# Seven-product weight groups in seven of eight places, and a down block's low part made by an accumulating GpSimd transfer

## The chip, the cores and the metric

The kernel runs on one core of one Trainium2 chip. The metric is the device time of one execution in microseconds (us). The engines are named as in the profile: PE is TensorE (PEld its weight loads), DVE is VectorE, ACT is ScalarE, POOL is GpSimd, SP is SyncE, which here only issues DMAs.

## What is computed

One decoder layer on 256 tokens of 2048 features, in float32: a SwiGLU with 5632 hidden features, a mixer of attention heads, and a second SwiGLU. The change touches the two SwiGLUs.

```python
def swiglu(x, w_gate, w_up, w_down):
    return (jax.nn.silu(x @ w_gate) * (x @ w_up)) @ w_down
...
h = h + 0.5 * swiglu(rms_norm(h, norm_ffn1_g[l]), ffn1_w_gate[l], ffn1_w_up[l], ffn1_w_down[l])
...
h = h + o @ w_out[l]
h = h + 0.5 * swiglu(rms_norm(h, norm_ffn2_g[l]), ffn2_w_gate[l], ffn2_w_up[l], ffn2_w_down[l])
```

## The kernel before

**A product.** A float32 value is kept as the sum of a rounded part ("hi", type fp32r) and what the rounding lost ("lo"). One product of a 128x128 block of activations with a 128x512 block of weights is three matmuls (`mm3`, lines 326 to 328): hi by hi, hi by lo, lo by hi. Weights arrive as float32, so each block of them has to be split: ACT casts it to hi, and DVE subtracts hi from the raw block to get lo.

**Units and down blocks.** A SwiGLU goes through 11 blocks of 512 hidden features. A *unit* (`unit`, line 589) computes gate and up of one block: it takes 8 weight groups of 128x2048, each 1 MB. A *down block* (`down`, line 679) takes 4 groups of 1 MB from `w_down` for one block and adds the result to h: ACT scales the sums into `st` (line 710), and GpSimd adds `st` to h in SBUF by an accumulating DMA of 512 KB (line 718). The order is unit 0, unit 1, down 0, unit 2, down 1, and so on; the last two down blocks are done together behind unit 10. A unit and the down block behind it are called a *round* here.

**Two kinds of groups.** A group of kind D (`whole`, line 391) is one load, one ACT cast and one DVE subtract of 128x2048, and 8 products. A group of kind S (`seven`, line 418) uses Winograd's form of a 2x2 block product: 7 products, for which DVE first forms sums of weight blocks (lines 437, 444, 445), ACT casts 1536 raw and 2048 summed columns in three pieces, and DVE subtracts twice (line 389, 1536 and 2048 columns). On the side of the activations the combinations are formed once for each pair of blocks (`form_of`, line 551) and kept in tiles `fu`. Behind a unit with S groups, DVE combines the sums in PSUM by eight operations of 128x512 (line 626), then comes the activation function (ACT, line 641, and DVE, line 649), the transposes (PE, line 507), and the split of the result into `hT` (ACT line 665, DVE line 389).

The table `UNITS` gives the kind of each group of each unit: 8 D in unit 0, then 3, 5, and from unit 3 on 6 S of 8.

**Buffers and order.** Three raw buffers of 1 MB (`raw` twice, and `rawx` in the first SwiGLU or `rawy` in the second), two for sums, five for hi and five for lo. An S group takes two of hi and two of lo, a D group one of each; a pair comes free when PE has used it. SP issues the loads in the order of the groups; a load waits until its raw buffer has been read for the last time.

The order of the instructions on every engine inside a SwiGLU is fixed by a planner (`arrange`, line 97): it goes through the tasks with a cost for each (`cast`, `sub`, numbers such as 0.69), a lag until the result can be used, and a due place counted in products, and writes down the order that comes out. The chip then waits on semaphores in that order; the costs themselves do nothing there.

Of the kernel before, what the change touches and what calls it, by code (L numbers as in the profile page):

```python
# [9 lines left out]
F32 = mybir.dt.float32  # L10
# [7 lines left out]
P = 128  # L18
# [25 lines left out]
F2_ORDER += [(2, "whiy", F32R)] * (NHI - 2 - FREE2) + [(3, "wloy", F32R)] * (NLO - 2 - FREE2) + [(0, "rawy", F32)] * (NRAW - 3)  # L44


# [30 lines left out]

LAG = 0.06
AHEAD = 60


def cast(n):
    return 0.2 + 0.00084 * n


def sub(n):
    return 0.16 + 0.00104 * n

# [8 lines left out]
def arrange(tasks, pools):  # L97
# [102 lines left out]
def hybrid_layer(ctx: ExitStack, tc: tile.TileContext, a: dict, out: bass.AP):  # L200
# [47 lines left out]
    cst = keep.tile([P, C_ONE], F32, name="cst")  # L248
    vec = keep.tile([P, V_END], F32, name="vec")
    pos = keep.tile([P, NT], I32, name="pos")  # L250

    hold.tile([P, 16], F32, name="pad")
    h = hold.tile([P, NT, D], F32, name="h")
    ident = cst[:, C_ID : C_ID + P]
    later = {}
    nc.scalar.dma_start(vec, a["vec"])

# [100 lines left out]
    def ffn(pool, u, wgu, wd, slots, banks, rstd, held=None, first=None, lead=None, done=None, out=None):  # L358
# [32 lines left out]
        def whole(src, pieces):  # L391
# [24 lines left out]
            return new, [(by[i * 512 // n], lambda i=i: cols(i)) for i in range(4)], {3: [("hi", c0), ("lo", l0)]}  # L416

        def seven(src):

# [48 lines left out]
        def group(kind, src, held, stat, need, form=None, pieces=1, last=False):  # L468

            new, w, free = seven(src) if kind == "S" else whole(src, pieces)  # L470
            n0 = len(main)
# [45 lines left out]
        def into_u(un, gcol, due):  # L517

            def finish(k, v, x):
                ends = []  # L520
                for j in range(2):
                    dst, gain = un(k + j), vec[:, gcol + k + j : gcol + k + j + 1]
                    c = task("act", 0.46, lambda j=j, dst=dst, gain=gain: nc.scalar.mul(dst[:, 0, :], v()[:, j], gain), [x], due)
                    l = task("dve", 0.48, lambda j=j, dst=dst, gain=gain: stt(
                        out=dst[:, 1, :], in0=v()[:, j], scalar=gain, in1=f32(dst[:, 0, :]), op0=ALU.mult, op1=ALU.subtract,
                    ), [c] + ends[-1:], due)
                    ends.append(l)
                    ready[k + j] = [c, l]
# [4 lines left out]
        def squares_of(ssq, c, need, due):  # L533

            ends = []
            for t in range(NT):
                q = task("act", 0.84, None, need[t], due, take={"sq": 1})
                q.give.append(("sq", q))
# [9 lines left out]
        forms = {}  # L548
        count = [k.count("S") for k in UNITS]

        def form_of(p, need, due):

            tile_, over = fu[p], u(2 * p)[:, :, P:SEQ]

# [34 lines left out]
        def unit(b):  # L589

            kinds, ns = UNITS[b], count[b]
            pair = {"S": iter(range(ns)), "D": iter(range(ns, 8))}
            held, hs, sq3 = {}, [], []
            for n, kind in enumerate(kinds):
                p = next(pair[kind])
                if b == 0 and first is not None:
                    first[0](p, task, ready)
                if kind == "S" and p not in forms:
                    fresh[p] = len(main)
                    form_of(p, used[p] + [x for k in (2 * p, 2 * p + 1) for x in ready.get(k, ())], len(main) - 4)  # L600
                n0 = group(
# [17 lines left out]
            if ns:  # L619
# [4 lines left out]
                def step(o_, key, in1, op, need, due, free=True):  # L624
                    return task(
                        "dve", 0.69, lambda: tt(out=o_(), in0=bank_of(held[key]), in1=in1(), op=op), need + [held[key]["last"]], due,
                        give=[("bank", held[key]["first"])] if free else (),
# [11 lines left out]
            for t in range(NT):  # L639
                src = (lambda t=t: s_tile()[:, t, :]) if ns else (lambda t=t: bank_of(R(t, 0)))  # L640
                a = task("act", 0.73, lambda t=t, src=src: nc.scalar.activation(
                    s_tile()[:, t, :], src(), AF.Silu, scale=rms[-1][:, t : t + 1]
# [6 lines left out]
                f = task("dve", 0.7, lambda t=t, src=src: stt(  # L649
                    out=s_tile()[:, t, :], in0=src(), scalar=rms[-1][:, t : t + 1], in1=s_tile()[:, t, :], op0=ALU.mult, op1=ALU.mult,  # L650
# [8 lines left out]
            def finish(k, v, x):  # L659
# [5 lines left out]
                c = task("act", cast(512), lambda: nc.scalar.copy(rows_tile()[:, :, 0, :], v()), [x], due + 4)  # L665
                l = task("dve", 0.69, lambda: low(rows_tile()[:, :, 1, :], v(), rows_tile()[:, :, 0, :]), [c], due + 4)
                row_ready[b, k // 2] = [c, l]
# [11 lines left out]
        def down(blocks, final):  # L679
# [21 lines left out]
        def settle(cp, held, final, later):  # L701

            due, c0, ends = len(main), 2 * cp * 512, []
            for t in range(NT):
                if not final:
                    pair = []
                    for j in range(2):
                        def run(t=t, j=j, pair=pair, held=held):
                            st = own("st", pair[0].got["st"][0], [P, 1024], F32)
                            nc.scalar.mul(st[:, j * 512 : j * 512 + 512], bank_of(held[t, j]), 0.5)  # L710
                        pair.append(task(
                            "act", 0.63, run, [held[t, j]["last"]] + pair, due + t + 4 * j, take={"st": 1} if j == 0 else (),
                            give=[("bank", held[t, j]["first"])],
# [100 lines left out]
    with tc.tile_pool(name="f1", bufs=1) as fp:  # L814
# [10 lines left out]
        def before(p, task, ready):  # L825
# [12 lines left out]
            for j in range(2):  # L838
                k = 2 * p + j
                gain = vec[:, V_G1 + k : V_G1 + k + 1]  # L840
                c = task("act", 0.46, lambda j=j, k=k, gain=gain: nc.scalar.mul(
                    u1(k)[:, 0, :], xs[i][:, p % 4, j], gain
                ), [ld], 8 * p - 4)
                l = task("dve", 0.48, lambda j=j, k=k, gain=gain: nc.vector.scalar_tensor_tensor(
                    out=u1(k)[:, 1, :], in0=xs[i][:, p % 4, j], scalar=gain, in1=f32(u1(k)[:, 0, :]),
# [32 lines left out]
    with tc.tile_pool(name="mix", bufs=1) as mp:  # L878
        ap_ = mp
        mst = mp.tile([P, C_END - C_ONE], F32, name="mst")  # L880
        nc.sync.dma_start(mst, a["cst"][:, C_ONE:])
        ones, tri = mst[:, :P], mst[:, C_TRI - C_ONE : C_TRI - C_ONE + P]
        m_swa, m_fox = (mst[:, C_MSK - C_ONE + i * SEQ :][:, :SEQ] for i in range(2))
# [54 lines left out]
        def rope_tables(name, gcol):  # L938
            g = vec[:, gcol : gcol + HD]
            ga = g[:, 0:32].unsqueeze(1).broadcast_to([P, NT, 32])  # L940
# [8 lines left out]
        nsink = ap_.tile([P, 32], F32, name="nsink")[:, :NH]  # L949
        nc.vector.tensor_scalar_mul(nsink, vec[:, V_SINK : V_SINK + NH], -1.0)  # L950

# [92 lines left out]
        def fox_mm(hf, i):  # L1044
# [10 lines left out]
        nc.vector.tensor_tensor(  # L1055
            out=z, in0=prs[:, :, 0:NH], in1=vec[:, V_BF : V_BF + NH].unsqueeze(1).broadcast_to([P, NT, NH]), op=ALU.add
        )
# [116 lines left out]
        def fox_rows(hf, i, pr, rf):  # L1174
# [3 lines left out]
            for t in range(NT):  # L1178
# [11 lines left out]
                for jj in range(2):  # L1190
                    bt = small_ps()
                    for j in range(4):
# [7 lines left out]
                        bt[0 : HD + 2, :].rearrange("p (j k) -> p j k", j=4),  # L1200
                        vec[0 : HD + 2, gcol : gcol + 1],
                    )
# [84 lines left out]
    with tc.tile_pool(name="f2", bufs=1, reuse_waits=REUSE) as fp:  # L1287
        slots, fu = [[], [], [], []], []
        for i, nm, dt in F2_ORDER:
            if i == 4:  # L1290
                fu += [fp.tile([P, 3, 2, P], F32R, name="fu%d" % p) for p in range(max(k.count("S") for k in UNITS))]
            else:
# [89 lines left out]
```

## Time and profile before

| what | us |
|---|---|
| median of 3 runs (lowest, highest) | 1747.77 (1747.45, 1747.9) |
| the profiled execution's own time | 1747.29 |
| its span, first to last instruction | 1745.0 |
| first SwiGLU, to its last transposes | about 0 to 684 |
| mixer | about 684 to 1054 |
| second SwiGLU | about 1054 to 1745 |

The span is what the profile covers; the 2.29 us around it are in the time alone. The page gives busy time by engine, a picture in 40 slices, the DMA queues, the chain of work that ended last, and the costliest groups of instructions. A busy PE is not a PE at its peak, since matmuls overlap: the distance from one start to the next is what counts. The same holds for DVE and ACT here, as the rows in the prediction show.

### The profile page before, as it was taken

Reading aid. Unit: us, or ns where it says so; the run is one execution under the profiler, and the core shown is the slowest. Engines: PE = TensorE matmul, PEld = TensorE weight load, DVE = VectorE, ACT = ScalarE, POOL = GpSimd, SP = SyncE. Lnnn points to the kernel's source line nnn. Section 1 sums busy time; section 2 is a strip of 40 time slices with the busy share of each in tenths; the row PEclk is TensorE's granted clock in tenths of the full one; section 3 lists DMA queues with packets and bytes.
Section 4 is the critical chain, followed back from the end, with each engine's and each line's share of the span. In section 5 each row is a group of like instructions: output and inputs, shape, how many; then the busy total and the mean of one; then the engine's idle time right before and its main releaser. Section 6 shows DMA issues by size and latency. Waiting matters only on the chain.

```text
span 1745.0 us, 21056 instructions
## 1 busy us (share of the span) xinstructions
PE 1734.7 (99%) x8052; PEld 1444.1 (83%) x8052; DVE 1510.2 (87%) x1640; ACT 1058.4 (61%) x1217; POOL 73.8 (4%) x94
## 2 busy tenths in 40 slices
PE   9999999999999999999999999999999999999999
PEld 6888888888888888998788888888888888888887
DVE  7899999998999996668777769799999999999994
ACT  7566566666666654655766656556666566656661
POOL 0000000000000000000000000000000000000000
PEclk9999999999999999999999999999999999999999
DMA  9676677678678664564444456577678578667763
GB/s 345 221 234 237 215 247 246 212 241 250 229 220 266 227 237 154 166 210 153 139 146 138 135 191 241 201 209 241 217 227 259 220 233 265 215 226 246 256 214 121
DMA packets 73141, 377.49 MB, mean 216 GB/s; under 512 B 7760, under 2 KB 16464, under 8 KB 39504
## 3 DMA queue, kind: packets, MB, share of 16 engines
q1 hardware_dynamic: 62064, 337.09, 53.8%
q0 software_dynamic: 10688, 38.80, 11.5%
q8 instruction: 63, 1.03, 0.2%
q14 instruction: 38, 0.31, 0.1%
q10 hardware_dynamic: 288, 0.25, 0.0%
HBM read 336.27 MB, written 2.10 MB: 194 GB/s over the span
## 4 chain that ended last, share of the span: by engine, by line
PE 98%; DMA 1%; DVE 0%; ACT 0%; issue 0%; SPq 0%; DVEq 0%
PE acc L327 25%; PE acc L326 25%; PE acc L328 25%; PE sm L328 6%; PE sm L326 6%; PE sm L327 6%; PE acc L507 1%; PE sm L1025 1%; PE sc L1214 1%; DMA rawx<-in_wgu 1%; PE sm L1031 1%; PE sm L1193 0%; PE sm L507 0%; DMA raw<-in_wgu 0%; PE sc L1139 0%; PE sm L1032 0%
## 5 line engine op out<-in xcount | busy, mean ns | idle before, releaser
L326 PE MATMUL acc<-whi,u 128*128 128x512 f32 (+1 forms) x690 | 263.4, 383 | 0.9 <-DVE s L989 0.9
L327 PE MATMUL acc<-wlo,u 128*128 128x512 f32 (+1 forms) x690 | 263.4, 382 | 0.6 <-DVE wlo L389 0.5
L328 PE MATMUL acc<-whi,u 128*128 128x512 f32 (+1 forms) x690 | 262.0, 381 | 0.0
L243 DVE TENSOR_TENSOR wlo<-raw,whi 128x1024 fp32r<-128x1024 f32 (+1 forms) x112 | 128.9, 1154 | 75.1 <-ACT whi L242 74.5
L242 ACT CAST whi<-raw 128x1024 fp32r<-128x1024 f32 (+1 forms) x112 | 111.0, 991 | 96.8 <-PE acc L328 88.1
L389 DVE TENSOR_TENSOR wlo<-raw,whi 128x1536 fp32r<-128x1536 f32 (+3 forms) x73 | 142.1, 1949 | 8.8 <-ACT whi L407 8.7
L326 PEld LDWEIGHTS acc<-whi,u 128*128 128x128 f32 x690 | 129.4, 188 | 24.0 <-DVE s L989 1.3
L327 PEld LDWEIGHTS acc<-wlo,u 128*128 128x128 f32 x690 | 129.5, 188 | 23.4 <-DVE wlo L389 1.4
L328 PEld LDWEIGHTS acc<-whi,u 128*128 128x128 f32 x690 | 129.4, 188 | 22.1 <-issue 0.8
L710 ACT ACTIVATE st<-acc 128x512 f32<-128x512 f32 x109 | 65.5, 601 | 82.3 <-PE acc L328 81.2
L389 DVE TENSOR_TENSOR wloy<-raw,whiy 128x1536 fp32r<-128x1536 f32 (+1 forms) x55 | 110.2, 2004 | 5.5 <-ACT whiy L407 5.5
L718 POOL DMA_DIRECT2D h<-st x72 | 62.4, 867 | 1212.8 <-ACT st L710 1110.0
L389 DVE TENSOR_TENSOR wlox<-raw,whix 128x2048 fp32r<-128x2048 f32 (+1 forms) x52 | 109.5, 2111 | 1.0 <-ACT whix L407 1.0
L389 DVE TENSOR_TENSOR wlo<-sums,whi 128x2048 fp32r<-128x2048 f32 x45 | 102.9, 2286 | 8.3 <-ACT whi L425 8.3
L437 DVE TENSOR_TENSOR sums<-raw 128x1024 f32<-128x1024 f32 x76 | 92.6, 1219 | 14.9 <-DMA raw<-in_wgu 14.9
L407 ACT CAST whi<-raw 128x2048 fp32r<-128x2048 f32 (+2 forms) x43 | 75.3, 1752 | 36.1 <-DMA raw<-in_wd 15.7
L407 ACT CAST whix<-raw 128x2048 fp32r<-128x2048 f32 x35 | 66.9, 1911 | 39.4 <-DMA raw<-in_wd 11.8
L327 PE MATMUL acc<-wlox,u 128*128 128x512 f32 x223 | 86.9, 390 | 0.5 <-DVE wlox L389 0.5
L328 PE MATMUL acc<-whix,u 128*128 128x512 f32 x223 | 86.8, 389 | 0.0
L326 PE MATMUL acc<-whix,u 128*128 128x512 f32 x223 | 86.8, 389 | 0.0
L389 DVE TENSOR_TENSOR wloy<-sums,whiy 128x2048 fp32r<-128x2048 f32 x34 | 77.7, 2286 | 4.4 <-ACT whiy L425 4.4
L327 PE MATMUL acc<-wloy,u 128*128 128x512 f32 x209 | 81.4, 390 | 0.1
(340 smaller groups left out, 4526.5 us busy)
## 6 DMA issues: line engine op xcount, KB each, us to landing
raw<-in_wgu SPq DMA_DIRECT2D x109, 1024.0 KB, 5.1
raw<-in_wd SPq DMA_DIRECT2D x65, 1024.0 KB, 4.8
h<-st POOLq DMA_DIRECT2D x72, 512.0 KB, 6.0
rawy<-in_wgu SPq DMA_DIRECT2D x33, 1024.0 KB, 4.8
rawx<-in_wgu SPq DMA_DIRECT2D x32, 1024.0 KB, 5.8
raw<-in_wf SPq DMA_DIRECT2D x48, 512.0 KB, 3.8
raw<-in_wo SPq DMA_DIRECT2D x32, 512.0 KB, 3.4
raw<-in_ws SPq DMA_DIRECT2D x32, 388.0 KB, 3.5
```

The source lines that it names most:

```text
L242: nc.scalar.copy(hi, src)
L243: nc.vector.tensor_tensor(out=lo, in0=src, in1=hi.bitcast(F32), op=ALU.subtract)
L326: nc.tensor.matmul(o, lhsT=shi, rhs=mhi, start=start, stop=False)
L327: nc.tensor.matmul(o, lhsT=shi, rhs=mlo, start=False, stop=False)
L328: nc.tensor.matmul(o, lhsT=slo, rhs=mhi, start=False, stop=stop)
L389: tt(out=o_, in0=a, in1=f32(b), op=ALU.subtract)
L407: c.run = lambda raw=raw, hi=hi: nc.scalar.copy(hi(), raw())
L437: tt(out=sm()[:, :1024].rearrange("p (j n) -> p j n", j=2), in0=v[:, 0:3:2, :], in1=v[:, 3:4, :].broadcast_to([P, 2, 512]), op=ALU.add,)
L507: nc.tensor.transpose(bt[:, j * SEQ + t * P : j * SEQ + (t + 1) * P], src()[:, t, m], ident)
L710: nc.scalar.mul(st[:, j * 512 : j * 512 + 512], bank_of(held[t, j]), 0.5)
L718: nc.gpsimd.dma_start(h[:, t, c0 : c0 + 1024], st, accum_op=ALU.add)
L1025: nc.tensor.transpose(bt[:, j * P : (j + 1) * P], src[:, j, :], ident)
```

## The change

Seven edits go together.

1. `UNITS` now has a table for each SwiGLU: 4, 6 and then 7 S groups in the first, 5, 6 and then 7 in the second. The number of `fu` tiles goes from 6 to 7.
2. The third group of each down block but the last two gets a new kind, L (`added_low`): ACT casts the raw block to hi and so frees the raw buffer; ACT writes minus hi into lo; a DMA from GpSimd then reads the same weight block from HBM a second time and adds it to lo in SBUF. DVE does nothing for this group.
3. The planner's costs for ACT and DVE are set lower, its general lag from 0.06 to 0.13.
4. The planner may take POOL's tasks out of order.
5. Room for the larger tiles: the scratch of GpSimd's DMAs goes from 2048 to 512 bytes of each partition, `vec` keeps only its first 64 columns, and the others (attention gains, sinks, forget bias) are loaded into a tile `own` of the mixer by one more DMA.
6. A padding tile goes from 16 to 56 columns.
7. Pairs of blocks are dealt to S and D groups through a table `PAIRS`, which leaves them as they were.

```diff
-UNITS = ["D" * 8, "DDSSDSDD", "DSSSSSDD"] + ["SDSSSSSD"] * (NB - 3)
+UNITS = [["D" * 8, x, "DSSSSSSD"] + ["SSSDSSSS"] * (NB - 3) for x in ("DDSSDSSD", "DSSDSSSD")]
+DOWN = "DDLD"
+PAIRS = [list(range(8)), list(range(8))]
...
-SCRATCH = 2048
+SCRATCH = 512
...
-LAG = 0.06
+LAG = 0.13
...
-    return 0.2 + 0.00084 * n
+    return 0.04 + 0.00087 * n
...
-    return 0.16 + 0.00104 * n
+    return 0.07 + 0.00104 * n
...
-            some = left[:1] if e in ("sp", "pool") else [t for t in left if t.due <= pos + AHEAD]
+            some = left[:1] if e == "sp" else [t for t in left if t.due <= pos + AHEAD]
...
+        def added_low(src):
+
+            ld = task("sp", 2.9, lambda: nc.sync.dma_start(raw(), src), take={"raw": 1}, lag=2.3)
+            c = task("act", cast(2048), lambda: nc.scalar.copy(hi(), raw()), [ld], take={"hi": 1}, give=[("raw", ld)])
+            n = task("act", cast(2048), lambda: nc.scalar.mul(lo(), f32(hi()), -1.0), [c], take={"lo": 1})
+            a = task("pool", 0.9, lambda: nc.gpsimd.dma_start(lo(), src, accum_op=ALU.add), [n], lag=9)
...
+            return [(ld, -45), (c, -20), (n, -20), (a, -20)], w, {3: [("hi", c), ("lo", n)]}
...
-                    "D", wd[cp][2 * b + c], held[cp], lambda k, t, b=b, c=c: halves(rows[b][:, 2 * c + k], t),
+                    "D" if final else DOWN[i], wd[cp][2 * b + c], held[cp], lambda k, t, b=b, c=c: halves(rows[b][:, 2 * c + k], t),
...
+        own = mp.tile([P, V_END - V_BF], F32, name="own")
+        nc.sync.dma_start(own, a["vec"][:, V_BF:])
```

How the order moves is shown at three places of the first SwiGLU; numbers behind a name tell the buffers apart.

The first is DVE where the first groups of unit 7 are prepared. Before, from the low part that frees `rawx0` to the next sum formed from that buffer:

```order
L389 TENSOR_TENSOR wlox0_93<-rawx0_87,whix0_90 128x1536
L389 TENSOR_TENSOR wlox1_94<-sums0_88,whix1_91 128x2048
L389 TENSOR_TENSOR wlox2_95<-raw0_70,whix2_92 128x2048
L437 TENSOR_TENSOR sums1_89<-raw1_71 128x1024
L437 TENSOR_TENSOR sums0_88<-rawx0_87 128x1024
```

and now, where line 392 is the old 389, and 450, 457, 458 are the old 437, 444, 445:

```order
L392 TENSOR_TENSOR wlo0_74<-rawx0_87,whi0_72 128x1536
L450 TENSOR_TENSOR sums0_88<-raw1_71 128x1024
L392 TENSOR_TENSOR wlo1_75<-sums1_89,whi1_73 128x2048
L457 TENSOR_TENSOR sums0_88<-sums0_88,raw1_71 128x512
L458 TENSOR_TENSOR sums0_88<-sums0_88,raw1_71 128x512
L450 TENSOR_TENSOR sums1_89<-rawx0_87 128x1024
```

Between the reading that frees `rawx0` and the next one from it stood two subtracts of 2048 columns and a sum; now there are one subtract, a sum and the two short sums.

The second is ACT at the turn from unit 7 to the down block behind it, now; line 410 is the cast of a D group (old 407), 636 copies a sum out of PSUM, 424 and 425 are the new group's cast and negation, 655 is the activation function:

```order
L410 CAST whix1_91<-raw1_71 128x2048
L410 CAST whix2_92<-raw0_70 128x2048
L636 COPY s_455<-sm_120 128x512
L424 CAST whi0_72<-rawx0_87 128x2048
L425 ACTIVATE wlo0_74<-whi0_72 128x2048
L410 CAST whi1_73<-raw1_71 128x2048
L655 ACTIVATE s_455<-s_455,rmy_420 128x512
```

Before, the down block's four casts stood there alike, with no negation, and DVE had a subtract for each of the four; now DVE has three.

The third is POOL's program for the first three rounds, now (without buffer numbers):

```order
L426 DMA wlox_93<-in_wd 128x2048
L732 DMA h<-st 128x1024 x4
L426 DMA wlo_74<-in_wd 128x2048
L732 DMA h<-st 128x1024 x4
L426 DMA wlox_95<-in_wd 128x2048
L732 DMA h<-st 128x1024 x4
```

Before, only the rows `h<-st` stood there, four to a round; the new transfer is now the first of its round.

More of the change, by code (lines that the diff above doesn't have):

```diff
@@ L416, in whole @@
             return new, [(by[i * 512 // n], lambda i=i: cols(i)) for i in range(4)], {3: [("hi", c0), ("lo", l0)]}
+        def added_low(src):
[3 more added lines that the diff above has]
+            a = task("pool", 0.9, lambda: nc.gpsimd.dma_start(lo(), src, accum_op=ALU.add), [n], lag=9)
+            raw, hi, lo = lambda: raws[ld.got["raw"][0]], lambda: his[c.got["hi"][0]], lambda: los[n.got["lo"][0]]
+            w = [([c, a], lambda i=i: (cols_of(hi())[i], cols_of(lo())[i])) for i in range(4)]
+            return [(ld, -45), (c, -20), (n, -20), (a, -20)], w, {3: [("hi", c), ("lo", n)]}
         def seven(src):
@@ L468, in group @@
         def group(kind, src, held, stat, need, form=None, pieces=1, last=False):
-            new, w, free = seven(src) if kind == "S" else whole(src, pieces)
+            new, w, free = seven(src) if kind == "S" else added_low(src) if kind == "L" else whole(src, pieces)
             n0 = len(main)
@@ L536, in squares_of @@
             for t in range(NT):
-                q = task("act", 0.84, None, need[t], due, take={"sq": 1})
+                q = task("act", 0.74, None, need[t], due, take={"sq": 1})
                 q.give.append(("sq", q))
@@ L548, in ffn @@
         forms = {}
-        count = [k.count("S") for k in UNITS]
+        units = UNITS[0 if first is not None else 1]
+        count, seven_of = [k.count("S") for k in units], PAIRS[0 if first is not None else 1]
         def form_of(p, need, due):
-            tile_, over = fu[p], u(2 * p)[:, :, P:SEQ]
+            tile_, over = fu[seven_of.index(p)], u(2 * p)[:, :, P:SEQ]
             def views(a):
@@ L589, in unit @@
         def unit(b):
-            kinds, ns = UNITS[b], count[b]
-            pair = {"S": iter(range(ns)), "D": iter(range(ns, 8))}
+            kinds, ns = units[b], count[b]
+            pair = {"S": iter(sorted(seven_of[:ns])), "D": iter(sorted(seven_of[ns:]))}
             held, hs, sq3 = {}, [], []
             for n, kind in enumerate(kinds):
-                p = next(pair[kind])
+                p = next(pair["D" if kind == "L" else kind])
                 if b == 0 and first is not None:
@@ L599, in unit @@
                     fresh[p] = len(main)
-                    form_of(p, used[p] + [x for k in (2 * p, 2 * p + 1) for x in ready.get(k, ())], len(main) - 4)
+                    form_of(p, used.get(p, []) + [x for k in (2 * p, 2 * p + 1) for x in ready.get(k, ())], len(main) - 4)
                 n0 = group(
@@ L625, in step @@
                     return task(
-                        "dve", 0.69, lambda: tt(out=o_(), in0=bank_of(held[key]), in1=in1(), op=op), need + [held[key]["last"]], due,
+                        "dve", 0.605, lambda: tt(out=o_(), in0=bank_of(held[key]), in1=in1(), op=op), need + [held[key]["last"]], due,
                         give=[("bank", held[key]["first"])] if free else (),
@@ L711, in settle @@
                         pair.append(task(
-                            "act", 0.63, run, [held[t, j]["last"]] + pair, due + t + 4 * j, take={"st": 1} if j == 0 else (),
+                            "act", 0.51, run, [held[t, j]["last"]] + pair, due + t + 4 * j, take={"st": 1} if j == 0 else (),
                             give=[("bank", held[t, j]["first"])],
@@ L938, in rope_tables @@
         def rope_tables(name, gcol):
-            g = vec[:, gcol : gcol + HD]
+            g = own[:, gcol - V_BF : gcol - V_BF + HD]
             ga = g[:, 0:32].unsqueeze(1).broadcast_to([P, NT, 32])
@@ L949, in hybrid_layer @@
         nsink = ap_.tile([P, 32], F32, name="nsink")[:, :NH]
-        nc.vector.tensor_scalar_mul(nsink, vec[:, V_SINK : V_SINK + NH], -1.0)
+        nc.vector.tensor_scalar_mul(nsink, own[:, V_SINK - V_BF : V_SINK - V_BF + NH], -1.0)
         def softmax_pv(scores, mask, vals, dst, nsk=None, paired=False):
@@ L1055, in hybrid_layer @@
         nc.vector.tensor_tensor(
-            out=z, in0=prs[:, :, 0:NH], in1=vec[:, V_BF : V_BF + NH].unsqueeze(1).broadcast_to([P, NT, NH]), op=ALU.add
+            out=z, in0=prs[:, :, 0:NH], in1=own[:, :NH].unsqueeze(1).broadcast_to([P, NT, NH]), op=ALU.add
         )
@@ L1200, in fox_rows @@
                         bt[0 : HD + 2, :].rearrange("p (j k) -> p j k", j=4),
-                        vec[0 : HD + 2, gcol : gcol + 1],
+                        own[0 : HD + 2, gcol - V_BF : gcol - V_BF + 1],
                     )
@@ L1290, in hybrid_layer @@
             if i == 4:
-                fu += [fp.tile([P, 3, 2, P], F32R, name="fu%d" % p) for p in range(max(k.count("S") for k in UNITS))]
+                fu += [fp.tile([P, 3, 2, P], F32R, name="fu%d" % p) for p in range(max(k.count("S") for k in UNITS[1]))]
             else:
```

21 lines of the change are left out of this document (11 added, 10 removed).

## Prediction

> **What bounds the kernel now.** I read the page first: busy time by engine, then the chain of work that ended last.
>
> ```profile
> PE 1734.7 (99%) x8052; PEld 1444.1 (83%) x8052; DVE 1510.2 (87%) x1640; ACT 1058.4 (61%) x1217; POOL 73.8 (4%) x94
> PE 98%; DMA 1%; DVE 0%; ACT 0%; issue 0%; SPq 0%; DVEq 0%
> ```
>
> PE has work in 99% of the span and makes 98% of the chain, so a matmul that goes away is time that goes away, as long as nothing else comes last. DVE at 87% is an average over stages. The windows of two rounds, one in each SwiGLU, show what it is where the change is made (columns: stretch, its length, then busy time of PE, PEld, DVE, ACT, POOL, each with its count, granted clock, DMA share, GB/s):
>
> ```profile
> 352.00:414.10 62.10, 62.10 (x280) 51.53 (x279) 58.69 (x49) 39.27 (x37) 3.44 (x4) 1.00 0.75 237
> 1394.20:1456.30 62.10, 62.10 (x281) 51.53 (x279) 58.69 (x49) 39.41 (x37) 3.48 (x4) 1.00 0.74 237
> ```
>
> A steady round lasts 62.10 us. PE never stops in it, the clock is full, and DVE has 3.41 us to spare (62.10 - 58.69). The kernel is bound by PE, with DVE close behind; that small reserve is what the change spends.
>
> **What goes: 63 matmuls.** The first SwiGLU had 3 + 5 + 8 x 6 = 56 S groups and gets 4 + 6 + 8 x 7 = 66; the second gets 5 + 6 + 56 = 67. That is 21 groups with one product less, 63 matmuls. Their price comes from the timeline of PE, first and last row of 42 in sequence:
>
> ```profile
> 380.59 0.39 PE L326 MATMUL acc<-whix,u 128*128 128x512 f32 x1
> ...
> 389.88 0.39 PE L328 MATMUL acc<-whix,fu 128*128 128x512 f32 x1
> ```
>
> 41 steps in 9.29 us are 0.2266 us a matmul (the 0.39 overlap), 0.68 a product. So PE loses 63 x 0.2266 = **14.3 us**, 0.68 of it in each round from unit 3 on: 62.10 becomes 61.42.
>
> **What comes to DVE.** Its rows overlap too, so I take steps from one start to the next:
>
> ```profile
> 312.92 2.29 DVE L389 TENSOR_TENSOR wlox<-sums,whix 128x2048 fp32r<-128x2048 f32 x1
> 315.12 0.68 DVE L444 TENSOR_TENSOR sums<-sums,raw 128x512 f32<-128x512 f32 x1
> 315.84 0.69 DVE L445 TENSOR_TENSOR sums<-sums,raw 128x512 f32<-128x512 f32 x1
> 316.45 1.22 DVE L437 TENSOR_TENSOR sums<-raw 128x1024 f32<-128x1024 f32 x1
> 317.59 1.75 DVE L389 TENSOR_TENSOR wlox<-raw,whix 128x1536 fp32r<-128x1536 f32 x1
> 319.25 2.29 DVE L389 TENSOR_TENSOR wlox<-sums,whix 128x2048 fp32r<-128x2048 f32 x1
> ```
>
> A low part of 2048 columns costs 2.20, the short sums 0.72 and 0.61, the long sum 1.14, a low part of 1536 columns 1.66. An S group is 6.33 in all, a D group 2.20. A steady round trades a D for an S (+4.13) and drops one subtract for the L group (-2.20): 58.69 + 1.93 = **60.62 us**. Against PE's 61.42, **0.80 us** are left of 3.41. There are 14 such rounds with a down block behind the unit, 7 in each SwiGLU.
>
> So the question is how long DVE waits in a round. It cannot run freely: in the order that I read, its low parts for the seven groups end, counted from that of the first, up to 5.6 us later than PE needs them (up to the last one 7 x 6.33, plus 2.20 for the D group, less the sums of the first two groups, which are formed ahead, 2 x 2.47, 41.6 us in all, against 53 products, 36.0 us), so it must enter a unit that far ahead; and the first row that combines the unit's sums needs product 56 (38.1 us) and stands two subtracts further on, at 46.0 us, so it can be at most 7.9 ahead. The room is 2.3 us.
>
> **The waits of DVE.** Its longest waits, in the stretches from 227.8 to 662.9 and from 1144 to 1643 us:
>
> ```profile
> DVE sums L437 <- DMA rawx<-in_wgu: 14.6, 7, 3.1
> DVE hT L389 <- ACT hT L665: 3.8, 7, 0.6
> ...
> DVE sums L437 <- DMA raw<-in_wgu: 13.0, 6, 3.3
> ```
>
> One wait of some 2.1 us in a round (14.6 / 7, 13.0 / 6), always for a load. In the round of the quoted rows it looks like this:
>
> ```profile
> 295.38 0.33 SPq L420 DMA_DIRECT2D rawx<-in_wgu  x1
> 302.44 1.23 DVE L437 TENSOR_TENSOR sums<-rawx 128x1024 f32<-128x1024 f32 x1 [1.59 <-DMA rawx<-in_wgu]
> DMA to landing us min/median/max: 4.8/5.5/7.0
> ```
>
> The load is issued when DVE has read the buffer for the last time, and DVE comes back after two subtracts and a sum, 2 x 2.20 + 1.14 = 5.5 us; the load takes 7.06. The last row is that of the loads into `rawx` in the round from 290 to 352: the quickest landed in 4.8. Now DVE comes back after 2.20 + 1.14 + 0.72 + 0.61 = 4.67 us, so the wait lies between 0.2 (a load of 4.8) and 2.4 (one of 7.06). What made that load slow stands on POOL's queue:
>
> ```profile
> 290.88 0.86 POOL L718 DMA_DIRECT2D h<-st  x1 [46.68 <-ACT st L710]
> 294.49 0.86 POOL L718 DMA_DIRECT2D h<-st  x1 [2.75 <-ACT st L710]
> ```
>
> Two accumulating transfers had been issued 4.5 and 0.9 us ahead of it. In the new order the load follows the second group's low part instead of the first's, some 5 us later in the round, when these two are mostly through and the next two have only begun. I take 0.9, nearer the free load, and for the waits on `hT` 0.2 of the 0.54 (3.8 / 7), since two sums now stand ahead of them. DVE's round becomes 60.62 + 1.1 = 61.7, 0.3 above PE's: 14 x 0.3 = **4.2 us** that PE stands.
>
> **The L group.** From the page, the answer on line 718 (the transfers `h<-st`), the groups by shape and the chain of waits in order of time:
>
> ```profile
> q0 software_dynamic: 10688, 38.80, 11.5%
> L718 POOL DMA_DIRECT2D h<-st x72: 851/860/1027, 105.0 to 1658.1; - x72
> DMA to landing us min/median/max: 4.5/6.0/9.2
> L407 ACT CAST whix<-raw 128x2048 fp32r<-128x2048 f32 x35 | 66.9, 1911 | 39.4 <-DMA raw<-in_wd 11.8 <-PE acc L328 10.3 <-issue 8.1
> L423 ACT CAST whi<-sums 128x1024 fp32r<-128x1024 f32 x45 | 47.4, 1053 | 21.5 <-PE acc L328 11.3 <-DVE sums L437 6.8 <-PE sm L328 2.9
> L421 ACT CAST whi<-raw 128x1536 fp32r<-128x1536 f32 x30 | 44.5, 1483 | 21.1 <-PE sm L328 7.8 <-PE acc L328 3.8 <-ACT whix L425 2.2
> 1144.47 0.87 PE acc L507 x8
> ```
>
> 11.5% of 1745.0 us for 38.80 MB is 5.2 us a MB, so the 1.05 MB of an L take 5.4 us of all DMA engines, 2.7 more than an `h<-st`. No such transfer from HBM is in the trace; I bound its landing by these rows with 2.7 added: 7.2 to 11.9, and take 8.7. Its chain starts when unit 7's (or another's) last S group frees its raw buffer, at the latest 33.8 us into the unit (36.0 less a subtract): load 4.8, cast 1.9, negation 1.9 (as the cast; not in the trace, 1.05 to 2.3 by ACT's cast of 1024 columns and DVE's longest subtract), transfer 8.7 give 51.1. PE needs it behind 73 products and the transposes, 73 x 0.68 + 0.87 = 50.5. It is 0.6 late with DVE at its latest, and in time once DVE uses its room of 2.3. I cost it at **0**; the cover is that room.
>
> The Trainium skill, "DMA: Bandwidth & Descriptors", section "Anatomy of one DMA — SWDGE (gpsimd) path", fits 2.0 us plus bytes / 436e3 to one transfer of this path; an L would land in 4.4 us by that (an estimate), and never be late. The 6.0 measured for half the bytes speaks against using it for accumulating transfers; the sum is the same by both, though by the page the second rival below would lose its chance. The Trainium skill, "SBUF — State Buffer", section "SBUF: two separate sides", warns that a DVE operation in a two-port mode keeps GpSimd from writing descriptors; an L would then be late by up to one DVE operation, and that rival would gain. The 72 issues took 851 to 1027 ns beside a DVE that was 94% busy, so nothing of the kind shows here.
>
> **The rest.** ACT gets 3.6 us for the S group (1.5 + 2 x 1.05) less 1.9 for the D, and 1.9 for the negation: 39.3 + 3.6 = 42.9 of 61.4, no bound. POOL gets 18 issues of 0.86, with nothing else queued there but `h<-st`, which comes later in the round. SP gets one small load in the mixer, 0.33 us ahead of loads that are issued several groups early.
>
> The rounds of units 1 to 3 get three more S groups in the first SwiGLU and four in the second, and three L groups and one more combination in `fu` each. Their windows, first and last of three in each SwiGLU:
>
> ```profile
> 42.00:103.00 61.00, 61.00 (x279) 50.68 (x278) 54.74 (x58) 36.05 (x30) 0.00 (x0) 1.00 0.64 232
> ...
> 165.00:227.80 62.80, 62.80 (x279) 51.96 (x279) 58.48 (x54) 38.74 (x38) 3.44 (x4) 1.00 0.69 215
> 1082.00:1144.50 62.50, 62.50 (x282) 51.84 (x281) 51.10 (x44) 33.46 (x27) 0.00 (x0) 1.00 0.55 199
> ...
> 1206.00:1270.00 64.00, 64.00 (x288) 53.08 (x287) 59.70 (x55) 39.98 (x40) 3.44 (x4) 1.00 0.69 219
> ```
>
> DVE has 4 to 11 us to spare in each of these; the first SwiGLU's three rounds get 3 x 4.13 - 3 x 2.20 and about 2 for the combination (some six short rows), 8 us in all. On the whole it fits, but unevenly; I take 1.3 us of standing, from 0 to 6.
>
> **The sum**, against the profiled execution's own 1747.29 (0.5 below the median of the runs): 1747.3 - 14.3 + 4.2 + 1.3 = 1738.5, I say **1739**.
>
> **Rivals.**
> *Slower: the load that DVE waits for.* If the load is as slow as before, the wait is 2.4 and DVE's round 63.0, 1.6 above PE: 14 x 1.6 = 22.4, and 3 in the early units: 1747.3 - 14.3 + 25.4 = **1758**. The wait decides: from 1.7 us a round (0.80, and 14.3 - 1.3 over 14 rounds) the change costs time. For it speaks that the wait was there in 13 of 14 rounds and its reserve has shrunk from 5.5 to 4.67; against it, that these loads move past the slow transfers. With an L's 5.4 us before them the queue may be longer, too.
> *No change: the L lands late.* At 11.9 it is 3.8 late, 1.5 after the room. That lateness passes through DVE to the next unit's combinations, two rounds of work, so about half of it, 0.7, shows in each round: 18 x 0.7 = 12.6, and 1747.3 - 14.3 + 12.6 + 1.3 = **1747**. For it: a landing of 9.2 was seen for half the bytes.
> *The change does not do what it says:* the built program has 63 matmuls less and 18 transfers more, so this is left with almost nothing.
>
> **How the numbers follow.** Forecast 0.52 (1733 to 1744: all waits gone is 1733.0, waits of 1.5 are 1744); no change 0.20 (1744 to 1751); slower 0.27 (1751 to 1770, around 1758); other 0.01. A measurement of this kernel can tell 0.2%, 3.5 us, from nothing. Faster 0.54, same 0.19, slower 0.27. The range leaves out the top of the slower case: 1733 to 1763.
>
> **What would show it.** PE's windows: rounds of 61.4 to 61.7 if right, 62.1 for no change, 63 for the slower rival. DVE in them 60.6 busy; if not, the price of S is wrong. The wait of line 450 on a load: about 0.9 a round, or 2.4. PE's waits: on DVE's lo for the first rival, on the GpSimd transfer for the second; and the landing of line 426, 8.7 or 12.

## The result, and the profile after

| | before | after |
|---|---|---|
| median, us (lowest, highest) | 1747.61 (1747.21, 1747.9) | 1821.2 (1816.65, 1822.83) |
| profiled execution, us | 1747.29 | 1822.65 |
| its span, us | 1745.0 | 1820.8 |
| mean granted clock | 1.000 | 0.989 |

The ratio is 1.0417, with a 95% interval from 1.0397 to 1.0438: the change costs 74 us, where 9 us less were forecast. The page of after, busy time, GpSimd's DMA queue and the chain of work that ended last:

```profile
PE 1752.1 (96%) x7989; PEld 1440.4 (79%) x7989; DVE 1563.5 (86%) x1722; ACT 1119.5 (61%) x1281; POOL 90.5 (5%) x112
...
q0 software_dynamic: 13280, 57.68, 16.1%
...
PE 57%; DMA 15%; issue 13%; DVE 11%; ACT 3%; POOL 0%; SPq 0%; POOLq 0%; ACTq 0%; DVEq 0%
```

PE has 63 matmuls less, but it now makes 57% of the chain and no longer 98%; the rest is DMAs, DVE, and "issue", time in which an engine waited for nothing that the profile shows. The seven steady rounds of each SwiGLU (unit 3's transposes to unit 10's), first two rows of before, then two of after; columns: stretch, its length, busy time of PE, PEld, DVE, ACT and POOL, clock, DMA share, GB/s:

```profile
227.63:662.29 434.66, 434.66 (x1948) 360.64 (x1947) 410.58 (x337) 274.51 (x258) 24.18 (x28) 1.00 0.73 237
1269.86:1704.51 434.65, 434.65 (x1947) 360.64 (x1946) 410.56 (x337) 274.77 (x258) 24.22 (x28) 1.00 0.73 237
```

```profile
241.05:704.48 463.43, 440.95 (x1924) 360.14 (x1922) 426.20 (x357) 294.55 (x276) 29.80 (x34) 0.98 0.77 236
1320.14:1781.82 461.68, 439.80 (x1927) 359.55 (x1926) 424.96 (x357) 295.45 (x277) 29.80 (x34) 0.99 0.77 236
```

A round went from 62.09 to 66.1 us (925.11 / 14). DVE's work in it is 60.8, as forecast (60.62), but DVE is now idle for 5.3 us of it (925.11 - 851.16, by 14), and PE no longer works without a stop. What they wait for, in the waits of after (engine, line, releaser: us in all, times, longest):

```profile
POOL h L732 <- issue: 234.9, 37, 12.6
...
ACT st L724 <- DMA h<-st: 60.1, 19, 7.7
...
DVE sums L450 <- DMA rawx<-in_wgu: 24.9, 14, 2.8
...
DVE sums L450 <- DMA rawy<-in_wgu: 24.0, 14, 3.2
...
PE acc L330 <- DMA wlo<-in_wd: 14.4, 6, 3.1
PE acc L330 <- DMA wlox<-in_wd: 13.3, 6, 3.7
...
PE acc L330 <- DMA wloy<-in_wd: 12.4, 5, 3.5
```

PE stands 40 us for the L transfers, 17 of 18 times. DVE waits for loads at line 450 (the old 437), as before. New is POOL, which waits 235 us for "issue" ahead of `h<-st`, something that the waits of before don't have. POOL's timeline in one round of after shows what it is:

```profile
497.81 0.89 POOL L426 DMA_DIRECT2D wlo<-in_wd  x1 [34.82 <-ACT wlo L425]
510.49 0.87 POOL L732 DMA_DIRECT2D h<-st  x1 [11.79 <-ACT whix L438]
515.20 0.86 POOL L732 DMA_DIRECT2D h<-st  x1 [3.84 <-issue]
522.22 0.89 POOL L732 DMA_DIRECT2D h<-st  x1 [6.16 <-issue]
527.37 0.87 POOL L732 DMA_DIRECT2D h<-st  x1 [4.27 <-ACT whix L438]
```

The answer on line 426 gives the landing of the L transfers, in all 18:

```profile
DMA to landing us min/median/max: 10.5/12.1/13.4
```

By the trace's records of the DMAs, the L issued at 497.81 landed at 510.18, and the three transfers behind it at 514.89, 521.91 and 527.06. Each next one is issued 0.3 us after the one before has landed: only one transfer of GpSimd is under way at a time. It is so in the whole trace: none of the 90 was issued before the one ahead of it had landed. Before, the two at 290.88 and 294.49 were issued 3.6 us apart and took 5.7 and 6.0, and 38 of the 72 were issued while the one ahead was still under way. The edit that could do this is the scratch of GpSimd's DMAs, 512 bytes for 2048; the first experiment tests it.

### The profile page after: what moved, and what is told of

Its sections match the earlier page's. It is cut to its first block, busy times and chain, and to the rows that moved or that the text cites. A ratio compares the mean times of both kernels' runs of the same rounds, so it can differ in the third digit from the quotient of the medians.

```text
span 1820.8 us, 21142 instructions
## 1 busy us (share of the span) xinstructions
PE 1752.1 (96%) x7989; PEld 1440.4 (79%) x7989; DVE 1563.5 (86%) x1722; ACT 1119.5 (61%) x1281; POOL 90.5 (5%) x112
## 4 chain that ended last, share of the span: by engine, by line
PE 57%; DMA 15%; issue 13%; DVE 11%; ACT 3%; POOL 0%; SPq 0%; POOLq 0%; ACTq 0%; DVEq 0%
PE acc L330 15%; PE acc L329 15%; PE acc L331 15%; DMA h<-st 3%; PE sm L330 3%; PE sm L329 3%; DVE wlo L392 3%; PE sm L331 3%; DMA wlox<-in_wd 3%; DMA wloy<-in_wd 3%; DVE wloy L392 3%; DMA raw<-in_wgu 2%; DMA wlo<-in_wd 2%; DVE wlox L392 2%; DVE sums L450 1%
## 5 line engine op out<-in xcount | busy, mean ns | idle before, releaser
L330 PE MATMUL acc<-wlo,u 128*128 128x512 f32 (+1 forms) x645 | 246.5, 383 | 1.9 <-DVE wlo L392 1.9
L329 PE MATMUL acc<-whi,u 128*128 128x512 f32 (+1 forms) x645 | 246.0, 383 | 1.4 <-DVE s L1005 0.9
L331 PE MATMUL acc<-whi,u 128*128 128x512 f32 (+1 forms) x645 | 244.5, 381 | 0.0
L392 DVE TENSOR_TENSOR wlo<-raw,whi 128x2048 fp32r<-128x2048 f32 (+3 forms) x77 | 148.9, 1938 | 12.0 <-ACT whi L434 7.5
L392 DVE TENSOR_TENSOR wlo<-sums,whi 128x2048 fp32r<-128x2048 f32 x53 | 121.1, 2284 | 9.9 <-ACT whi L438 9.8
L392 DVE TENSOR_TENSOR wloy<-raw,whiy 128x2048 fp32r<-128x2048 f32 (+1 forms) x54 | 109.7, 2037 | 7.3 <-ACT whiy L410 3.7
L330 PE MATMUL acc<-wlo,hT 128*128 128x512 f32 x230 | 93.6, 407 | 14.4 <-DMA wlo<-in_wd 14.4
L438 ACT CAST whi<-sums 128x1024 fp32r<-128x1024 f32 x53 | 55.8, 1054 | 77.2 <-DVE sums L458 65.0
L392 DVE TENSOR_TENSOR wloy<-sums,whiy 128x2048 fp32r<-128x2048 f32 x42 | 95.9, 2283 | 1.5 <-ACT whiy L438 1.5
L329 PE MATMUL acc<-whi,hT 128*128 128x512 f32 x230 | 93.3, 406 | 4.0 <-DVE sqh L640 3.9
L331 PE MATMUL acc<-whi,hT 128*128 128x512 f32 x230 | 92.7, 403 | 0.0
L392 DVE TENSOR_TENSOR wlox<-sums,whix 128x2048 fp32r<-128x2048 f32 x38 | 86.8, 2283 | 1.9 <-ACT whix L438 1.8
```

The lines of the kernel that those rows point to most:

```text
L329: nc.tensor.matmul(o, lhsT=shi, rhs=mhi, start=start, stop=False)
L330: nc.tensor.matmul(o, lhsT=shi, rhs=mlo, start=False, stop=False)
L331: nc.tensor.matmul(o, lhsT=slo, rhs=mhi, start=False, stop=stop)
L392: tt(out=o_, in0=a, in1=f32(b), op=ALU.subtract)
L438: cb = task("act", cast(1024), lambda: nc.scalar.copy(hs()[:, 1024:], sm()[:, 1024:]), [b, ca])
```

## The experiments

Times are medians; each ratio is to the old kernel on the same chip in the same job, with its 95% interval.

### The scratch

The changed kernel with a larger scratch, every instruction in its old place; and the old kernel with the small one.

```diff
-SCRATCH = 512
+SCRATCH = 1024
```

> The changed kernel with 1024 instead of 512 bytes of scratch for GpSimd's transfers, its instruction order being the same. Theory R (the smaller scratch lets GpSimd keep only one transfer in flight, so each h<-st waits until the one before has landed, st and the PSUM banks come free late and ACT stands): the 235 us that POOL sits before h<-st for no visible reason fall below 80, ACT's 60 us of waiting for h<-st below 15, and the time falls by 25 us or more, to 1795 or less. Theory L (PE stands at the accumulated low part, which lands 12.1 us after its issue, and the clock is halved behind such a stand): the landing stays at 11 to 12.5 and the time within 10 us of 1821. Theory D (DVE is the bound through S groups and late loads): the same, within 10 us of 1821.

Measured: 1789.84 us, ratio 1.0237 (1.0218 to 1.0256), 31 less than the changed kernel, as theory R had it. POOL's waits for "issue" are gone (all 72 are for ACT now), those of PE for an L fell from 40.1 to 31.3:

```profile
POOL h L732 <- ACT st L724: 383.2, 72, 13.2
...
PE acc L330 <- DMA wlox<-in_wd: 13.0, 6, 3.8
...
PE acc L330 <- DMA wloy<-in_wd: 9.2, 5, 3.8
PE acc L330 <- DMA wlo<-in_wd: 9.1, 6, 2.9
```

> The kernel before with 512 instead of 2048 bytes of scratch, nothing else. Theory R: the second h<-st of each pair is issued only when the first has landed, about 2.5 us later than now; the kernel before has slack there, so 1748 to 1756, and POOL's waits without a visible reason become some 100 us. Theories L and D: 1747 to 1748, and no such waits.

Its edit is `SCRATCH = 512` in the old kernel. Measured: 1761.72 us, ratio 1.0103 (1.0067 to 1.0138). The runs scatter from 1757.0 to 1776.1, and the profiled one is the longest. In it POOL waits 215.9 us for "issue", 27 times, no transfer is issued before the one ahead has landed, ACT waits 99.8 us for `st` to be read (2.3 before), and PE waits for ACT. Theory R had the mechanism, but too small: it expected 1748 to 1756 and some 100 us. So the small scratch alone costs 14 us in the old kernel and 31 in the new one, which has more and longer transfers to put one behind another. Is 1024 enough?

> The changed kernel with the old table of units (3, 5 and then 6 S groups) but with the L groups, and with 2048 bytes of scratch. DVE then has 56.5 us of work in a round of 62.1. Theory L: PE still stands 2 to 4 us at each of the 18 transfers and the clock drops behind it: 1785 to 1815. Theory R: the ring is as large as before, so 1746 to 1755. Theory D: DVE has more reserve than before, 1745 to 1750.

> Old table of units with L groups, scratch 1024 instead of 2048; same order otherwise. If 1024 is enough for this traffic (an L and h<-st two at a time), 1749 to 1753 as with 2048 (1750.1), and theory R needs nothing beyond 512 against 1024. If the ring still holds up the transfers, 1758 or more, and part of what is left in the kernel with 1024 and seven S groups is still the ring.

Both are the changed kernel with the old table of six S groups; one has 2048 and one 1024. Measured: 1750.07 (1.0013, 1.0004 to 1.0022) and 1750.21 (1.0014, 1.0004 to 1.0024): the same. Seven `fu` tiles leave no room for 2048, so the runs below with seven S groups stand on 1024.

### The L groups

```diff
-DOWN = "DDLD"
+DOWN = "DDDD"
```

> The changed kernel with plain groups in place of the 18 accumulated ones (scratch 512, seven S groups of eight; the order is planned anew). Theory L: what the L groups cost goes and DVE gets 2.2 us a round more, 62.8 us against PE's 61.4: 1760 to 1775. Theory D: DVE is the bound more than ever, 1821 plus 18 x 2.2, so 1840 to 1865. Theory R: h<-st is alone on the ring again, as in the kernel before with 512: 1755 to 1780.

> Seven S groups of eight without L groups, scratch 1024: the S groups alone. Theory L (with 1024 the late transfer sets the rounds: PE waits for it, the unit's combinations come late, and so the next unit): without it DVE alone counts, 62.8 us of work and some waits in a round of 61.4: 1760 to 1780, under the 1790 with L. Theory D (DVE with its work and its waits for loads sets the rounds): 2.2 us more work a round than with L and no relief: 1800 to 1820.

> The changed kernel with 1024 bytes of scratch and the L group as the fourth instead of the third of each down block, so that PE needs it 8 products (5.4 us) later, while its raw buffer comes free some 4 us later. Theory L: PE's waits for the transfer fall from 31 us to 10 to 20, and the time by 5 to 20, to 1770 to 1785. Theory D: the time stays within 5 us of 1790, since DVE has the same work.

> Old table of units, no L groups, scratch 2048: what is left of the change are the planner's new costs, POOL's tasks out of order, and the moved tiles. All theories: 1746 to 1750. If it is 1752 or more, the new costs of the planner or the moved tiles cost something of their own.

Measured: without L 1822.41 at 512 (1.0425, 1.0409 to 1.0442) and 1813.46 at 1024 (1.0378, 1.0361 to 1.0394), where with L it was 1789.84. With L as the fourth group (`"DDDL"`) 1825.57 (1.0443, 1.0428 to 1.0459), which no theory had: PE waits 33 us for L all the same, and ACT 124 us for `st`. With six S groups and no L, 1756.32 (1.005, 1.0035 to 1.0065). At 512 no theory had 1822; at 1024 theory D had 1813 in its range.

So with the larger scratch the L groups, late as they are, save 24 us where there are seven S groups, and 6 where there are six; at 512 they save 1. (The planner orders the instructions anew in each of these kernels, so its order is part of these differences.) Without them DVE has 2.2 us a round more to do, and most of it comes out: the steady rounds without L, at 1024, last 66.58 us, where with L they last 64.74 (906.33 / 14):

```profile
233.75:702.61 468.86, 443.37 (x1926) 358.56 (x1925) 441.39 (x366) 282.66 (x271) 23.48 (x27) 0.99 0.69 221
1310.94:1774.23 463.29, 440.99 (x1927) 357.94 (x1925) 441.11 (x366) 280.85 (x270) 23.47 (x27) 0.99 0.70 223
```

DVE works 63.04 us a round (882.50 / 14), and the round is 3.5 us longer than that. The last run also says that the edits apart from S, L and scratch (planner, tiles) cost 8.8 us by themselves, where all theories had 1746 to 1750; they were not separated further.

### DVE, the late transfer, or the loads

With the scratch out of the way 40 us stay between six S groups and seven. First the transfer alone is left out, then a little of DVE's work, in the kernel with the transfer and in the one without.

```diff
-            a = task("pool", 0.9, lambda: nc.gpsimd.dma_start(lo(), src, accum_op=ALU.add), [n], lag=9)
-            w = [([c, a], ...
+            w = [([c, n], ...
```

> The changed kernel with SCRATCH = 1024 (1789.8 us), without the accumulating transfer of the L groups: their low part stays minus the rounded block, so the low half of the block is left out of the result; all else, the load, the cast, the negation and the 63 matmuls less, stays. Theory 'late L' (PE stands because the L transfer lands late, 31.3 us in 17 waits, and the granted clock falls to half for some us after the longer of them, 0.8% of the span, 14 us): both go, 1789.8 - 31 - 14 = 1745, rounds of 61.5 to 62.3, clock above 0.998. Theory 'DVE' (seven S groups fill DVE, 60.6 us a round and some 3 us of waits for loads; the wait for L only shows what DVE would show elsewhere): 1780 to 1790, PE waits for DVE's low parts instead. In between, 1755 to 1775, both count, and the DVE share is the distance from 1745.

```diff
-            a.run, b.run = outer, inner
+            a.run, b.run = outer, (lambda: None) if AT[0] >= 3 and AT[1] in (2, 5) else inner
```

(`AT` holds the unit and the place of the group in it; `inner` is the two short sums.) In both edits the other instructions of DVE and ACT keep their order.

> The changed kernel with SCRATCH = 1024 (1789.8 us), in which two of the seven S groups of each unit from unit 3 on skip the two short sums of 512 columns (lines 457 and 458), so these columns of the sums are stale: 64 instructions of VectorE less, 42 us in all, 2.66 us a unit, with every other instruction in its old place. Theory 'DVE' (a round lasts as long as DVE's 60.6 us of work and its waits of 4 to 5 us, until PE's 61.4 is longer): 16 x 2.66 = 42 less, at the most down to what PE needs, 1747 (1743 to 1757). Theory 'late transfers' (the landing of the L and of the loads sets the round, whatever DVE has to do): 1780 to 1790.

> The same two pairs of short sums left out, in the kernel whose L groups have no accumulating transfer (1775.3 us; the low half of the block is left out). Theory 'DVE': 58.0 of work and 2.8 of waits are less than PE's 61.4, so PE bounds: 14 x 2 us less, 1745 (1741 to 1752). Theory 'late loads': the loads that DVE waits for are no earlier: 1768 to 1776.

Measured: without the transfer 1775.27 (1.0141, 1.0109 to 1.0172), 14.5 less; with the transfer and less work for DVE 1770.95 (1.0139, 1.0098 to 1.0179), 19 less; with both 1749.43 (1.0016, 0.9992 to 1.004), 26 less than with the first alone, its runs scattered from 1739.5 to 1760.9. The steady rounds of the kernel without the transfer, by windows:

```profile
234.32:677.94 443.62, 434.72 (x1924) 354.12 (x1923) 423.68 (x357) 293.36 (x276) 23.49 (x28) 1.00 0.72 230
1290.76:1736.13 445.37, 435.21 (x1926) 354.82 (x1925) 423.73 (x357) 294.85 (x277) 23.48 (x28) 1.00 0.72 229
```

the longest waits of DVE and of PE in the second of these stretches (lines 449, 662 and 639 are 450, 663 and 640 elsewhere; 639 is the combining of a unit's sums):

```profile
DVE sums L449 <- DMA rawy<-in_wgu: 16.3, 7, 4.2
DVE s L662 <- ACT s L654: 3.1, 9, 0.7
...
PE acc L329 <- DVE sqh L639: 8.9, 6, 1.6
```

and the same windows of the kernel with less work for DVE besides:

```profile
235.43:669.44 434.01, 431.02 (x1923) 355.55 (x1922) 405.59 (x329) 294.65 (x276) 23.50 (x28) 1.00 0.74 234
1275.36:1705.27 429.91, 429.91 (x1926) 356.56 (x1925) 405.93 (x329) 296.28 (x277) 23.44 (x28) 1.00 0.74 237
```

Without the transfer the clock is full and the round is 63.50: DVE's 60.53 and 2.97 of idle time, 2.3 of which (16.3 / 7) is the wait for one load. PE stands 10.2 us in that stretch (445.37 - 435.21), 8.9 of them until DVE has combined sums. With 2.6 us less to do, DVE still waits for that load (17.0 us in the same seven rounds), but the round of the second SwiGLU is 61.42 and PE never stops; in the first SwiGLU it is 62.0. So it is not the load's lateness as such: it is DVE's work and its waits together against PE's 61.42. Theory "late loads" falls, theory "DVE" holds for these rounds, and theory "late L" has 14.5 us, the transfer's traffic and the clock lost behind PE's stands included. With the transfer (1770.95), "DVE" had expected 1743 to 1757: part of L's lateness stays even when DVE has room, since PE still waits 18.8 us for L.

### The order

> SCRATCH = 1024, and in the L group the negated rounding is written first, straight from the raw block, and the rounded part second: the transfer can be issued one cast, 1.9 us, earlier, and nothing is added or left out. Theory 'late L': each of the 15 waits in steady rounds (0.8 to 4.0 us) gets 1.9 us shorter, 9 us of 31 stay, and part of the 14 us of lost clock comes back: 1789.8 - 22 - 6 = 1762 (1755 to 1770). Theory 'DVE': 1785 to 1795, with PE waiting for DVE's low parts in place of L.

```diff
+            n = task("act", cast(2048), lambda: nc.scalar.mul(lo(), raw(), -1.0), [ld], take={"lo": 1})
+            c = task("act", cast(2048), lambda: nc.scalar.copy(hi(), raw()), [ld, n], take={"hi": 1}, give=[("raw", ld)])
```

> SCRATCH = 1024, seven S groups and L as in the changed kernel, but with the planner's old figures for the cost of each instruction (LAG 0.06, casts 0.2 + 0.00084 n and so on). The planner only sets the order of the instructions. Theory 'planner' (the new figures make an order that suits the chip worse; without seven S groups and L the other edits cost 8.8 us): 1775 to 1783. Theories 'late L' and 'DVE': 1785 to 1795, since neither the L chain nor DVE's work changes.

> SCRATCH = 1024, and the planner counts 13 us instead of 9 from the issue of an L transfer to its landing (11.9 measured); only the order of instructions changes. Theory 'late transfers': the order now puts L's chain or what PE does ahead of it where it fits: the 31 us of waits for L shrink to under 15, 1765 to 1780. Theory 'DVE': the waits only move to DVE's low parts: 1782 to 1800.

> SCRATCH = 1024, L groups as in the changed kernel, seven S groups only in units 3, 5, 7 and 9 of each SwiGLU, six in 4, 6, 8 and 10 (24 matmuls come back, 5.4 us). Six S groups throughout with L gave 1750, seven 1790. If each unit with seven costs by itself (the L or the loads late in that round, whatever DVE did before): half way, 1770. If DVE saves up in the round with six S groups (56.5 us of work in 62.1) what it lacks in the next: 1745 to 1755, and the waits for L go nearly everywhere.

In the last one `UNITS` alternates between the old and the new row from unit 3 on. In its units with six S groups the seventh pair's D group reads activations that `form_of` has overwritten, so that these products are not the reference's.

All four missed. The negation first: 1873.69 (1.0696, 1.0637 to 1.0755). PE's waits for L did shrink, from 31.3 to 19.8 where 9 were expected. But the raw buffer comes free one cast later, the planner's order changed with it, and DVE's waits for loads at line 450 rose from 37.6 us to 125.9, almost all of them these:

```profile
DVE sums L450 <- DMA rawy<-in_wgu: 64.8, 17, 6.4
DVE sums L450 <- DMA raw<-in_wgu: 56.1, 16, 6.2
```

The old costs: 1895.90 (1.0848, 1.0831 to 1.0865); PE waits 91 us for L, so the new costs of the planner, which only set an order, are worth 106 us here. The longer lag: 1812.80 (1.0381, 1.0362 to 1.04); PE's waits for L fell to 23 us, and others came for it, such as 12.2 us until DVE has combined sums. Alternating: 1789.79 (1.0244, 1.0228 to 1.026), as much as seven S groups throughout. Measured from PE's first matmul of one unit to that of the next, its rounds of units 3 to 9 last 62.1 to 64.0 us with six S groups and 62.8 to 68.4 with seven, so nothing shows that DVE saves up in one round for the next. These four have in common that the order of the whole stage changed; they say that it matters by up to 100 us, and nothing clean on one cost.

### Parts of the change in the old kernel

> The old kernel, with only the S groups of units 1 and 2 as in the change (4 and 6 in the first SwiGLU, 5 and 6 in the second, where 3 and 5 were), six in the later units as before, no L, SCRATCH 2048: 5 S groups more, 15 matmuls less, 3.4 us. DVE had 4 to 11 us to spare in these rounds. If its reserve is what decides: 1744.2 (1743 to 1745.5). If a round with one S group more costs by itself, as in the later units: 1748 to 1760.

> The old kernel with one S group more in unit 2 of each SwiGLU (six for five), nothing else: 6 matmuls less, 1.4 us. In early_before, where units 1 and 2 both had more, the round of unit 2 was 1.4 and 1.5 us shorter, and the round ahead of it lost 3.3 and 1.5. If the loss came from unit 1's new groups and the combinations formed for them: 1744.5 to 1746.5. If forming one more pair costs its own round what it saves: 1747 to 1750.

> The old kernel (six S groups, SCRATCH 2048, the planner's old costs, the old tiles in the mixer) with the L groups alone, and the rule for POOL's list that lets them go ahead of later transfers. DVE gets 16 x 2.2 us less to do. Theory 'DVE has reserve here, so that nothing is gained': 1746.5 to 1749. If the L lands late here too, or loads are late behind it: 1750 to 1760.

Measured: both early units with more S groups 1755.68 (1.0043, 1.0028 to 1.0058); unit 2 alone 1751.27 (1.0021, 1.0012 to 1.003); the L groups alone 1764.21 (1.0102, 1.0087 to 1.0118). All slower. With unit 2 alone, measured from transposes to transposes in the first SwiGLU, 62.77 us become 65.69 and the next 64.13 become 62.42, as if one round paid for the other. But the new order has the transposes of unit 2 3.4 us later in their down block, and this moves the boundary. Measured from PE's first matmul of one unit to that of the next, the round of unit 2 is shorter in both SwiGLUs, 62.29 us for 62.78 and 62.29 for 62.77; what is lost comes in later rounds whose groups did not change, 63.02 and 63.42 us in the longest of them (unit 6) for 62.1. Why those rounds are longer is open. With the L groups alone the other transfers of GpSimd land later. The landing of `h<-st` with them, by the answer on its line:

```profile
DMA to landing us min/median/max: 4.7/8.7/12.6
```

The median was 6.0 without them, and ACT waits 47.7 us for `st`, 2.3 before. In the old order the L groups cost 16.5 us; in the new one they saved 6 with six S groups and 24 with seven. No kernel that was run and leaves no work out was faster than the old one.

## Why the prediction was wrong

The spans of the profiled executions, cut into the 14 steady rounds and the rest:

| | 14 steady rounds | the rest | span |
|---|---|---|---|
| before | 869.3 | 875.7 | 1745.0 |
| forecast (1738.5 less 2.29) | 864.1 | 872.1 | 1736.2 |
| seven S, 1024, L without its transfer | 889.0 | 885.7 | 1774.7 |
| with the transfer | 906.3 | 880.5 | 1786.8 |
| scratch 512: the changed kernel | 925.1 | 895.7 | 1820.8 |

Line by line the miss of 85 us of span is 38 + 12 + 34. The 38 hold the new order of the instructions too, whose own price with seven S groups no run shows.

- **PE's matmuls: right.** A round of 61.42 was forecast; where nothing else bounds, it is 429.91 / 7 = 61.42.
- **DVE's work: right.** 60.62 forecast, 60.53 to 60.80 measured.
- **"I take 0.9, nearer the free load": wrong**, and so the step from 60.62 to 61.7. Even without any L transfer this wait is 2.3 us a round, the upper bound (2.4) that the text had and did not take; with all idle time DVE's round is 63.50. That is 889.0 - 864.1 = 25 us in the steady rounds. The first rival had this mechanism and nearly this price (63.0 a round); with it the change loses even where the scratch is mended and the transfer left out. The reserve of 4.67 us was right, but the load did not become quicker: it moved from behind one pair of `h<-st` to just ahead of the other, and landed no earlier. In the kernel without the transfer:

```profile
1301.10 0.33 SPq L432 DMA_DIRECT2D rawy<-in_wgu  x1
1301.75 0.87 POOL L731 DMA_DIRECT2D h<-st  x1 [5.39 <-ACT st L723]
1304.47 0.86 POOL L731 DMA_DIRECT2D h<-st  x1 [1.85 <-ACT st L723]
1308.81 1.23 DVE L449 TENSOR_TENSOR sums<-rawy 128x1024 f32<-128x1024 f32 x1 [3.07 <-DMA rawy<-in_wgu]
```

DVE came for the load 4.64 us after its issue, and it landed after 7.7. The next two rounds show the same, with landings of 6.7 and 8.8. That these transfers are what slows it was not tested. Of the 3.41 us that DVE was idle in a round of before, 2.97 stayed idle.
- **"I cost it at 0; the cover is that room": wrong.** The L landed in 12.1 us, not 8.7, past even the bound of 11.9 (11.9 in the median with the larger scratch), and the room of 2.3 did not cover it. PE stood 40 us in the changed kernel and 31 with the larger scratch; leaving the transfer out gives 12 us of span, 14.5 of the medians. In the 4.4 us of the prediction's estimate by the fit of the Trainium skill, "DMA: Bandwidth & Descriptors", section "Anatomy of one DMA — SWDGE (gpsimd) path", no L came; the shortest took 10.5 us. Of the wait that the Trainium skill, "SBUF — State Buffer", section "SBUF: two separate sides", warns of, the issues show nothing: the longest of the 18 took 1038 ns, as the longest of before (1027).
- **"POOL gets 18 issues of 0.86, with nothing else queued there but `h<-st`": the largest miss.** The fifth edit of the list, a scratch of 512 bytes, was never costed. It puts every transfer of GpSimd behind the landing of the one before, and the first of each round is the L of 12 us. 34 us of span, 31 of the medians.
- **"I take 1.3 us of standing, from 0 to 6" for the early rounds: too little.** Outside the steady rounds 3.6 us less were forecast; without the transfer it is 10 us more. In PE's rows of that kernel, unit 2 was as short as forecast (39.44 us in both SwiGLUs), but unit 3, the first with seven S groups, took 42.75 and 43.93 us, where 38.76 are enough in its quickest units.
- **The range** ended at 1763, with one rival's price. The mechanisms were priced as alternatives, but they came together, and their prices added up.

What is not settled: why the planner's other edits cost 8.8 us with six S groups, and what order would suit seven S groups and L best. A fourth raw buffer, which might take the load's wait away, was not tried.

## What to carry to other kernels

Idle time of the second busiest engine may be no reserve when it consists of waits in a loop with a buffer: look at what each of its waits hangs on before spending it, and take the wait as it stands in the trace unless a row shows it shorter. When a load moves away from slow transfers, look at which ones it moves to. Cost every edit of a diff, the ones that only make room above all; a resource that sets how many transfers are under way belongs to the price of each transfer. To tell a cost from the order that it came with, take single instructions out with all others left in place.

## What the hardware showed besides

With 512 bytes of scratch one GpSimd transfer was under way at a time, in the old kernel and in the new. With 1024, 57 of the 90 were issued while the one ahead was under way, and POOL waited only for what it was to transfer.

This stand of PE cost more than its length. At 510.22 PE had waited 2.49 us for an L. The windows from there on (clock is the third column from the end):

```profile
505.00:510.00 5.00, 2.73 (x17) 2.01 (x15) 3.49 (x6) 2.63 (x4) 0.00 (x0) 1.00 0.99 280
510.00:511.00 1.00, 0.78 (x3) 0.65 (x4) 1.00 (x2) 1.00 (x3) 0.51 (x1) 0.86 0.70 295
511.00:512.00 1.00, 1.00 (x4) 0.81 (x3) 1.00 (x3) 1.00 (x2) 0.36 (x1) 0.50 0.19 45
512.00:513.00 1.00, 1.00 (x4) 0.71 (x4) 1.00 (x1) 0.78 (x1) 0.00 (x0) 0.50 1.15 229
513.00:514.00 1.00, 1.00 (x4) 0.81 (x3) 1.00 (x2) 0.00 (x0) 0.00 (x0) 0.50 1.00 201
514.00:515.00 1.00, 1.00 (x6) 0.82 (x5) 1.00 (x1) 0.32 (x1) 0.00 (x0) 0.93 0.75 156
```

The granted clock falls to half for some 3.4 us once PE has begun again, and from 511.26 to 513.82 PE's matmuls start 0.43 us apart instead of 0.23. The mean of 0.989 over 1820.8 us is 20 us of full clock that were not granted; with the larger scratch 0.992, without the L transfer 1.000. The Trainium skill, "TensorE: Matmul & The Clock Gate", section "Part 1: The HAM clock gate", has the same half rate and a window of about 3.4 us, after an idle window of that length; here a stand of 2.49 us on one row was enough.
